# Seven of a layer's sixteen up-projection units computed as seven block products, with the order of the MLP and the home of its side sums changed

## The chip, the cores and the metric

The kernel runs on one core of one Trainium2 chip. The metric is the device time of one execution in microseconds (us). Before the change it is 1293.06 us, the median of three runs from 1291.07 to 1293.43.

## The reference

The reference is a decoder trunk of two layers on 512 tokens of width 1024, in float32. Each layer mixes tokens by attention, then applies a squared-ReLU MLP, then a gated input:

```python
hn = rmsnorm(h, norm_mlp_g[i])
u = jnp.square(jax.nn.relu(hn @ w_mlp_up[i]))      # 1024 -> 4096
h = h + u @ w_mlp_down[i]                          # 4096 -> 1024
gate = jax.nn.sigmoid(rmsnorm(h, norm_ple_g[i]) @ w_ple_gate[i])
h = h + (p[i] @ w_ple_proj[i]) * gate
```

The change lies in the MLP alone, and in a small regrouping of the attention's scratch columns.

## The kernel before, in words

The activations stand transposed: `h[0]` to `h[7]` are eight tiles of 128 features x 512 tokens. Every float32 operand of a matmul is split in two fp32r parts, a high part (ScalarE, a copy) and a low part (VectorE, value minus high part), and each product is three matmuls: high by high, high by low, low by high (`mm3`, L140 to L145). Weights come through `wload` (L112) as 1 MB tiles `raw` (two buffers) and are split into `wh`/`wl` (three buffers each).

The MLP (`mlp`, L734) cuts the 4096 hidden features into four quarters `ch`, and each quarter into four units `c` of 256 features.

`up(ch, c)` (L741) multiplies 256 columns of the up weights with all eight input tiles: 2 x 8 x 3 = 48 matmuls of 512 columns. Then a chain follows in one tile `u` of 7 x 256 columns, of which there is **one buffer** (L747): VectorE applies ReLU and the norm's factor `rstd` (L762), ScalarE squares (L763), VectorE forms four sums and differences (L768, L770, L772), ScalarE takes the high part `uh` of all seven pieces (L774) and VectorE the low part `ul` (L775). The next unit can begin its `u` when `ul` is done.

`down(ch, c)` (L786) multiplies a quarter's hidden features with 256 output columns. It does a 2 x 2 block product with seven block products instead of eight (the Strassen-Winograd scheme): VectorE forms the weights' sums `s13` and `s24` (L799 to L804), they are split (L806), and 7 x 4 x 3 = 84 matmuls of 256 columns run against the seven pieces of `uh`/`ul`. Parts of the result that several outputs share are kept as side sums, eight tiles `sides` in on-chip memory, added up over the quarters by ScalarE and VectorE (`total`, L841) and spread over `h` at the end of the MLP (`side_sums`, L919). VectorE also adds two of the four banks into `h` (L882, L883).

The order of the work is the Tile framework's: it orders each engine's instructions when the kernel is built, in each engine's queue they then run strictly in that order. In the program, quarter `ch + 1` starts with one up unit ahead of quarter `ch`'s four down units, so that the down units never start right behind the last up unit they need (L930 to L937):

```python
for c in range(4):
    up(0, c)
for ch in range(1, NCH):
    up(ch, 0)
    for c in range(4):
        down(ch - 1, c)
    for c in range(1, 4):
        up(ch, c)
```

In the last quarter there is nothing left to put ahead. There `down(3, 0)` multiplies by three of the four hidden units first and by the fourth at the end (`ks`, L863).

Of the kernel before, what the change touches and what calls it, by code (L numbers as in the profile page):

```python
# [35 lines left out]
GROUPS = ((2, 3, 0, 1), (0, 1, 2, 3))  # L36

# [25 lines left out]
def trunk(  # L63
# [29 lines left out]
    def col(name="c"):  # L93
        return spool.tile([P, 1], F32, tag="col", name=nm(name), bufs=24)
# [22 lines left out]
    def wsplit(raw, i, nk, n, pool=None):  # L117
        bufs = 3 if pool is None else 4
# [21 lines left out]
    def mm3(acc, lh, ll, rh, rl, start, stop):  # L140
        mm = nc.tensor.matmul(acc, lh, rh, start=start, stop=False)  # L141
        if warm_end:
            order(mm.ins, warm_end.pop())
        nc.tensor.matmul(acc, lh, rl, start=False, stop=False)  # L144
        return mm.ins, nc.tensor.matmul(acc, ll, rh, start=False, stop=stop).ins  # L145
# [164 lines left out]
    blk0 = [tuple(wpool.tile([P, KT, P], F32R, tag=t, name=nm(t), bufs=3) for t in ("wh", "wl")) for _ in range(2)]  # L310
# [76 lines left out]
    def mixer(layer, norm, nxt):  # L387
# [156 lines left out]
        def soft(hd, bt, i, s):  # L544
# [3 lines left out]
            mn = col("mn")  # L548
# [34 lines left out]
        def attend(g, kind, v, heads):  # L583
# [6 lines left out]
            def weights(x, i, evict):  # L590
                n = P * (i + 1)
                if kind == "diff":
# [3 lines left out]
                    s, r = (spool.tile([P, 2], F32, tag="cols", name=nm("cols"), bufs=12) for _ in range(2))  # L596
                    e0, e1 = (soft(heads[2 * x + m], bias[x][m], i, s[:, m:m + 1]) for m in range(2))
# [7 lines left out]
                if kind == "dil":  # L605
                    if i == 0:
                        bias[x] = load_bias(4 * g + x)
                    s, r = col("s"), col("r")
                    e = soft(heads[x], bias[x], i, s)
# [122 lines left out]
    T1, B11, T3, B21, B22, T2, T4 = range(7)  # L732

    def mlp(layer, fpool, norm, nxt):  # L734
# [3 lines left out]
        sides = [[fpool.tile([P, S], F32, tag=f"side{x}{c}", name=nm("side"), bufs=1) for x in range(2)] for c in range(4)]  # L738
        hidden, spare, stages, b12, low, lows, high = {}, [], [], [], [], [], []

        def up(ch, c):  # L741
            blk = block(w_up[layer, 4 * ch + c], KT, P)
            accs = [ps_wide() for _ in range(2)]
            run(lin_units(accs, blk, ahl, 0, KT, ch == 0 and c == 0))
            if not rstd:
                rstd.append(norm.finish(use_tables(sig_tail) if layer == 0 else None))
            u = fpool.tile([P, 7, HW], F32, tag="u", name=nm("u"), bufs=1)  # L747
            if ch == NCH - 1:
                if c == 0:
# [36 lines left out]
        def down(ch, c):  # L786
# [15 lines left out]
            if last and c:  # L802
                order(sum2, hidden[ch, 3][2] if c == 1 else lows[-1])
# [126 lines left out]
        for c in range(4):  # L930
            up(0, c)
# [236 lines left out]
```

## Time and profile before

| | |
|---|---|
| median of three runs | 1293.06 us |
| the profiled execution | 1293.15 us |
| its span, first to last instruction | 1291.4 us |
| around the span | 1.75 us |
| mean granted TensorE clock | 0.998 |
| layer 0, from the span's start: first up unit's first matmul, first matmul behind the MLP | 270.39 us, 608.25 us |
| layer 1: the same | 895.28 us, 1233.30 us |

A group's row reads: line, engine, operation, result<-operands, then count, busy time, mean of one, and the idle time ahead of it with what ended it. In a row of the timeline the first number is the start, the second the duration (the duration reaches past the next start, since instructions overlap: the pace is read from start to start). TensorE's rows are PE, its weight loads PEld, VectorE DVE, ScalarE ACT, GpSimd POOL, SyncE's DMA queue SPq.

### The profile page before, as it was taken

To read this page: it belongs to the slowest core of one execution; us is meant where nothing else is said; L and a number is where in the kernel's file an instruction comes from. 1 tells how busy PE (TensorE), PEld (TensorE's weight loads), DVE (VectorE), ACT (ScalarE), POOL (GpSimd) and SP (SyncE) were. 2 spreads that over 40 slices of the span, in tenths; PEclk is the share of its full clock that TensorE was granted. 3 is DMA by queue.
4 is the path that set the end of the run, shared out by engine and by line. 5 is a ranking of instruction groups with operands and counts; after the bars stand their busy time and mean duration, and the time that the engine had idled before them with its cause. 6 is when DMAs were issued, how large, how long until landed. Compare 5 with 4: busy or idle time off the path is not lost.

```text
span 1291.4 us, 19228 instructions
## 1 busy us (share of the span) xinstructions
PE 1273.3 (99%) x7488; PEld 1121.0 (87%) x7488; DVE 1003.5 (78%) x1662; ACT 707.8 (55%) x1146; POOL 215.2 (17%) x187
## 2 busy tenths in 40 slices
PE   9999999999999999999999999999999999999997
PEld 7988887888988989989889888788899898898986
DVE  6788898688848869679767777887785885986976
ACT  5667868555535344355556666765553443534644
POOL 2443433500000000001033333222000000000202
PEclk9999999999999999999999999999999999999999
DMA  6421423222232322648332222212223223254751
GB/s 212 144 82 53 161 74 115 90 98 98 98 103 94 119 101 78 194 114 222 130 130 83 82 90 81 67 58 94 102 98 109 87 98 128 69 155 135 173 183 66
DMA packets 33851, 144.25 MB, mean 112 GB/s; under 512 B 3872, under 2 KB 4608, under 8 KB 21088
## 3 DMA queue, kind: packets, MB, share of 16 engines
q1 hardware_dynamic: 29104, 134.37, 30.8%
q0 software_dynamic: 4224, 7.87, 3.6%
q8 instruction: 59, 0.97, 0.3%
q10 hardware_dynamic: 432, 0.79, 0.2%
q14 instruction: 32, 0.26, 0.1%
HBM read 131.92 MB, written 6.37 MB: 107 GB/s over the span
## 4 chain that ended last, share of the span: by engine, by line
PE 84%; DVE 8%; ACT 4%; issue 2%; DMA 1%; SPq 0%; POOL 0%; DVEq 0%; ACTq 0%
PE mm L141 11%; PE mm L144 11%; PE mm L145 11%; PE sc L144 5%; PE sc L145 5%; PE sc L141 5%; PE tp L145 5%; PE pv L145 5%; PE pv L144 5%; PE pv L141 5%; PE tp L144 5%; PE tp L141 5%; PE pv L579 3%; PE tp L558 2%; PE tp L900 2%
## 5 line engine op out<-in xcount | busy, mean ns | idle before, releaser
L122 ACT ACTIVATE wh<-raw 128x1024 fp32r<-128x1024 f32 (+1 forms) x156 | 160.6, 1034 | 140.6 <-PE mm L144 53.1
L126 POOL TENSOR_TENSOR wl<-raw,wh 128x512 fp32r<-128x512 f32 (+1 forms) x132 | 179.8, 1383 | 298.4 <-ACT wh L122 294.6
L141 PE MATMUL mm<-hi,wh 128*128 128x512 f32 x472 | 186.3, 395 | 0.4 <-DVE tmp L495 0.4
L145 PE MATMUL mm<-hi,wl 128*128 128x512 f32 x472 | 184.7, 391 | 0.0
L144 PE MATMUL mm<-lo,wh 128*128 128x512 f32 x472 | 184.5, 391 | 0.0
L128 DVE TENSOR_TENSOR wl<-raw,wh 128x1024 fp32r<-128x1024 f32 x90 | 109.5, 1222 | 38.1 <-ACT wh L122 34.1
L145 PEld LDWEIGHTS mm<-hi,wl 128*128 128x128 f32 x472 | 88.6, 188 | 19.9 <-POOL wl L126 0.4
L141 PEld LDWEIGHTS mm<-hi,wh 128*128 128x128 f32 x472 | 88.7, 188 | 17.2 <-DVE tmp L495 0.8
L144 PEld LDWEIGHTS mm<-lo,wh 128*128 128x128 f32 x472 | 88.7, 188 | 15.7
L784 POOL DMA_DIRECT2D s<-in_w_down_dram x4 | 4.5, 1134 | 581.2 <-DMA s<-in_w_down_dram 290.2
L813 ACT ACTIVATE wh<-s 128x1024 fp32r<-128x1024 f32 x58 | 61.1, 1053 | 54.5 <-DVE s L800 14.9
L552 ACT ACTIVATE e<-e,mn 128x128 f32<-128x128 f32 (+3 forms) x96 | 53.8, 561 | 62.3 <-DVE mn L549 61.9
L775 DVE TENSOR_TENSOR ul<-u,uh 128x1792 fp32r<-128x1792 f32 x32 | 64.8, 2024 | 29.7 <-ACT uh L774 29.6
L814 DVE TENSOR_TENSOR wl<-s,wh 128x1024 fp32r<-128x1024 f32 x58 | 70.8, 1221 | 16.6 <-ACT wh L813 16.2
L774 ACT ACTIVATE uh<-u 128x1792 fp32r<-128x1792 f32 x32 | 54.5, 1702 | 45.5 <-DVE u L772 45.5
L763 ACT ACTIVATE u<-u 128x512 f32<-128x512 f32 x64 | 39.7, 626 | 68.3 <-DVE u L762 68.1
L141 PE MATMUL sc<-hi,wh 128*128 128x512 f32 x184 | 72.2, 392 | 0.5 <-ACT hi L187 0.5
L144 PE MATMUL sc<-lo,wh 128*128 128x512 f32 x184 | 72.0, 391 | 0.4 <-DVE lo L188 0.4
L145 PE MATMUL sc<-hi,wl 128*128 128x512 f32 x184 | 71.7, 390 | 0.0
L141 PE MATMUL mm<-wh,hi 128*128 128x256 f32 (+1 forms) x216 | 63.1, 292 | 0.0
L145 PE MATMUL mm<-wh,lo 128*128 128x256 f32 (+1 forms) x216 | 63.0, 292 | 0.0
L144 PE MATMUL mm<-wl,hi 128*128 128x256 f32 (+1 forms) x216 | 62.9, 291 | 0.0
(306 smaller groups left out, 3873.8 us busy)
## 6 DMA issues: line engine op xcount, KB each, us to landing
raw<-in_w_up_dram SPq DMA_DIRECT2D x32, 1024.0 KB, 4.9
raw<-in_w_down_dram SPq DMA_DIRECT2D x32, 1024.0 KB, 4.9
raw<-in_w_in_dram SPq DMA_DIRECT2D x23, 1024.0 KB, 4.9
raw<-in_w_gate_dram SPq DMA_DIRECT2D x8, 1024.0 KB, 5.4
bias<-urow SPq DMA_DIRECT2D x24, 256.0 KB, 3.9
raw<-in_w_outa_dram SPq DMA_DIRECT2D x8, 768.0 KB, 4.2
pj<-pjd SPq DMA_DIRECT2D x16, 256.0 KB, 4.7
raw<-in_w_proj_dram SPq DMA_DIRECT2D x2, 1024.0 KB, 4.9
```

The costliest lines, as they stand in the source:

```text
L122: act = nc.scalar.activation(hi, src, AF.Copy)
L126: nc.gpsimd.tensor_tensor(lo[:, kx], src[:, kx], hi[:, kx].bitcast(F32), op=ALU.subtract)
L128: last_low[:] = [nc.vector.tensor_tensor(lo, src, hi.bitcast(F32), op=ALU.subtract).ins]
L141: mm = nc.tensor.matmul(acc, lh, rh, start=start, stop=False)
L144: nc.tensor.matmul(acc, lh, rl, start=False, stop=False)
L145: return mm.ins, nc.tensor.matmul(acc, ll, rh, start=False, stop=stop).ins
L552: nc.scalar.activation(e[:, 0:n], e[:, 0:n], AF.Exp, scale=-1.0, bias=mn, accum_out=s)
L763: chain.append(nc.scalar.activation(ui, ui, AF.Square, scale=0.5).ins)
L774: nc.scalar.activation(uh, u, AF.Copy)
L775: part = nc.vector.tensor_tensor(ul, u, uh.bitcast(F32), op=ALU.subtract)
L813: high[:] = [nc.scalar.activation(hi, src, AF.Copy).ins]
L814: low[:] = [nc.vector.tensor_tensor(lo, src, hi.bitcast(F32), op=ALU.subtract).ins]
```

## The change

1. **Seven block products in seven up units.** The units of `SEVEN` (one in quarter 0, three in quarter 1, three in quarter 2) are computed by `up_products` with the scheme that `down` uses: weights' sums, splits of seven weight blocks, 84 matmuls of 256 columns in three accumulators, four copies out of them ("snaps") between the products, and adds on VectorE. Their weights are packed by `_pack4`.
2. **The inputs' combinations.** The scheme needs sums and differences of the input blocks, for each of four pairs of input tiles. `combine_inputs(m)` makes them once a layer, two pairs after `up(0, 0)` and two after `up(0, 1)`, in the tile `u` and its one buffer.
3. **Order.** All four up units of a quarter precede its four down units. The split `ks` of `down`'s first unit now holds in every quarter.
4. **Side sums.** In quarters 0 to 2, `total` copies a bank to a tile `e` (ScalarE) and a DMA from GpSimd's queue writes or adds it to `sides_d` in device memory; the last quarter loads the sums back. The two adds to `h` go the same way, as accumulating DMAs. The tile `e` has five buffers, which the splits of `w11` and the snaps use too.
5. **Buffers.** `wh`/`wl` four instead of three, `uh`/`ul` four instead of five; the attention's columns share tiles; the scratch for GpSimd's DMAs is halved. In the last quarter `down(3, 1)` forms `s13` on VectorE, not by DMA.

The diff, cut to its core:

```diff
+SEVEN = {(0, 2), (1, 0), (1, 1), (1, 2), (2, 0), (2, 1), (2, 2)}
...
+        def differences(u):
+            nc.vector.tensor_tensor(u[:, 0], u[:, 0], u[:, 1], op=ALU.subtract)
+            nc.vector.tensor_tensor(u[:, 1], u[:, 3], u[:, 1], op=ALU.subtract)
+            nc.vector.scalar_tensor_tensor(u[:, 3], u[:, 0], -1.0, u[:, 3], op0=ALU.mult, op1=ALU.subtract)
+            nc.vector.scalar_tensor_tensor(u[:, 2], u[:, 3], -1.0, u[:, 2], op0=ALU.mult, op1=ALU.subtract)
+        def combine_inputs(m):
+            u = fpool.tile([P, 7, HW], F32, tag="u", name=nm("u"), bufs=1)[:, 0:4]
+            for j in range(2):
+                k = 2 * m + j
+                nc.scalar.activation(
+                    u[:, 2 * j:2 * j + 2].rearrange("p a c -> p (a c)"), h[k], AF.Copy, scale=gcol(1, layer, k))
+            differences(u)
+            hi, lo = (fpool.tile([P, 4, HW], F32R, tag=f"{t}{m}", name=nm(t), bufs=1) for t in ("th", "tl"))
+            nc.scalar.activation(hi, u, AF.Copy)
+            nc.vector.tensor_tensor(lo, u, hi.bitcast(F32), op=ALU.subtract)
...
+        def up_products(ch, c, u):
+            rv, s13, s24, _ = quarter_sums(wload(w_up[layer, 4 * ch + c]), None)
+            w11 = split(rv[:, A11:A11 + 1])
+            w12 = split(rv[:, A12:A22 + 1])
+            w24 = split(s24)
+            w13 = split(s13)
...
+            product(run0, w11, 0, B11, True, True)
+            s1 = snap(0, run0)
+            product(first, w12, 0, B21, True, True)
+            product(run0, w24, 0, T2, False, True)
+            s2 = snap(1, run0)
+            nc.vector.tensor_tensor(u[:, B11], first, s1, op=ALU.add)
+            product(second, w13, 0, T1, True, True)
+            r5 = snap(2, second)
+            product(run0, w13, 1, T3, False, True)
+            s3 = snap(3, run0)
+            product(second, w24, 1, B22, False, True)
...
+            product(run0, w12, 1, T4, False, True)
...
+        def collect(dst, src, sign=1.0, add=True):
+            t = t2k("e")[:, 0:src.shape[-1]]
+            nc.scalar.activation(t, src, AF.Copy, scale=sign)
+            nc.gpsimd.dma_start(dst, t, **(dict(accum_op=ALU.add) if add else {}))
...
-            for ks in ((0, 1, 2), (3,)) if last and c == 0 else (range(4),):
+            for ks in ((0, 1, 2), (3,)) if c == 0 else (range(4),):
...
-            nc.vector.tensor_tensor(h[2 * c], h[2 * c], banks[2], op=ALU.add)
+            if last:
+                nc.vector.tensor_tensor(h[2 * c], h[2 * c], banks[2], op=ALU.add)
...
+            else:
+                collect(h[2 * c], banks[2])
+                collect(h[2 * c + 1][:, 0:HW], banks[3][:, 0:HW], -1.0)
...
-        for c in range(4):
-            up(0, c)
-        for ch in range(1, NCH):
-            up(ch, 0)
-            for c in range(4):
-                down(ch - 1, c)
-            for c in range(1, 4):
+        for ch in range(NCH):
+            for c in range(4):
                 up(ch, c)
+                if ch == 0 and c < 2 and SEVEN:
+                    for m in range(2):
+                        combine_inputs(2 * c + m)
...
+            if ch < NCH - 1:
+                for c in range(4):
+                    down(ch, c)
```

What the build makes of it shows in the engines' queues. VectorE, layer 0, from the end of the first up unit's chain on (`ul` with the lowest number) to the second's; `u_...` is always the one buffer, under a new number at each turn. Before:

```order
L775 TENSOR_TENSOR ul_624_3084<-u_622_3082,uh_623_3083 128x1792
L128 TENSOR_TENSOR wl_647_3241<-raw_645_3238,wh_646_3240 128x1024
L762 SCALAR_TENSOR_TENSOR u_632_3154<-sc_630_3104,rstd_574_2889 128x512
L762 SCALAR_TENSOR_TENSOR u_632_3154<-sc_631_3105,rstd_574_2889 128x512
L768 TENSOR_TENSOR u_632_3154<-u_632_3154 128x2x256
L770 SCALAR_TENSOR_TENSOR u_632_3154<-u_632_3154 128x256
```

Now, at the same place, with the chain of the second up unit (L843) behind two turns of the combinations:

```order
L858 TENSOR_TENSOR ul_567_3028<-u_568_3029,uh_566_3027 128x1792
L129 TENSOR_TENSOR wl_612_3291<-raw_610_3288,wh_611_3290 128x1024
L745 TENSOR_TENSOR u_569_3039<-u_569_3039 128x256
L746 TENSOR_TENSOR u_569_3039<-u_569_3039 128x256
L747 SCALAR_TENSOR_TENSOR u_569_3039<-u_569_3039 128x256
L748 SCALAR_TENSOR_TENSOR u_569_3039<-u_569_3039 128x256
L759 TENSOR_TENSOR tl_571_3047<-u_569_3039,th_570_3046 128x1024
L745 TENSOR_TENSOR u_572_3050<-u_572_3050 128x256
L746 TENSOR_TENSOR u_572_3050<-u_572_3050 128x256
L747 SCALAR_TENSOR_TENSOR u_572_3050<-u_572_3050 128x256
L748 SCALAR_TENSOR_TENSOR u_572_3050<-u_572_3050 128x256
L759 TENSOR_TENSOR tl_574_3058<-u_572_3050,th_573_3057 128x1024
```

Two more such turns (`u_585`, `u_588`) stand behind the second unit's chain, then the third up unit's turn, then the fourth's: eight turns of `u` where there were four.

TensorE, layer 0, where the third up unit begins. Before, its matmuls (accumulator `tp_640`) follow the second unit's (`sc_631`) in a row of 48 of 512 columns:

```order
L145 MATMUL sc_631_3105<-hi_600_2989,wl_629_3101 128x512
L141 MATMUL tp_640_3176<-hi_572_2885,wh_636_3168 128x512
L144 MATMUL tp_640_3176<-lo_573_2886,wh_636_3168 128x512
L145 MATMUL tp_640_3176<-hi_572_2885,wl_637_3169 128x512
L141 MATMUL tp_640_3176<-hi_576_2899,wh_636_3168 128x512
```

Now, behind its first two products (24 matmuls that need no combination), the third unit (`tp_605`, `pv_607`) needs the first pair's combination (`th_570`, `tl_571`), and the fourth unit (`pv_615`) is dealt in between:

```order
L146 MATMUL tp_606_3183<-hi_552_2942,wl_600_3171 128x256
L142 MATMUL tp_605_3182<-th_570_3046,wh_601_3174 128x256
L142 MATMUL pv_607_3184<-th_570_3046,wh_603_3178 128x256
L142 MATMUL pv_615_3298<-hi_524_2838,wh_611_3290 128x512
L145 MATMUL pv_615_3298<-lo_525_2839,wh_611_3290 128x512
L145 MATMUL tp_605_3182<-tl_571_3047,wh_601_3174 128x256
L146 MATMUL tp_605_3182<-th_570_3046,wl_602_3175 128x256
L145 MATMUL pv_607_3184<-tl_571_3047,wh_603_3178 128x256
L146 MATMUL pv_607_3184<-th_570_3046,wl_604_3179 128x256
L146 MATMUL pv_615_3298<-hi_524_2838,wl_612_3291 128x512
```

The second, third and fourth pairs' parts (`th_573`, `th_586`, `th_589`) follow in the same manner, each ahead of what is queued behind it; all of the fourth unit and 12 matmuls of the first down unit stand between them. The third unit's last 36 matmuls, and with them its `uh`/`ul`, stand behind the fourth pair.

More of the change, by code (lines that the diff above doesn't have):

```diff
@@ L547, in soft @@
             e = t2k("e")
-            mn = col("mn")
             nc.vector.tensor_tensor_reduce(
@@ L732, in trunk @@
     T1, B11, T3, B21, B22, T2, T4 = range(7)
+    A12, A22, A21, A11 = range(4)
+    sides_d = dpool.tile([DEPTH, 4, 2, P, S], F32, tag="sides", name="sides")
     def mlp(layer, fpool, norm, nxt):
@@ new lines, in mlp @@
+        hidden, sides, b12, low, lows, high, combos = {}, {}, [], [], [], [], []
+        def differences(u):
[13 more added lines that the diff above has]
+            nc.vector.tensor_tensor(lo, u, hi.bitcast(F32), op=ALU.subtract)
+            (h0, l0), (h1, l1) = ahl[2 * m], ahl[2 * m + 1]
+            left, right = slice(0, HW), slice(HW, S)
+            combos.append({T1: (hi[:, 0], lo[:, 0]), T3: (hi[:, 1], lo[:, 1]), T4: (hi[:, 2], lo[:, 2]), T2: (hi[:, 3], lo[:, 3]),
+                           B11: (h0[:, left], l0[:, left]), B21: (h1[:, left], l1[:, left]), B22: (h1[:, right], l1[:, right])})
@@ new lines, in split @@
+        def split(src):
+            n = src.shape[1]
+            if n == 2:
+                hi, lo = (wpool.tile([P, 2, 4, P], F32R, tag=t, name=nm(t), bufs=4) for t in ("wh", "wl"))
+            else:
+                hi, lo = (t2k("e", dtype=F32R).rearrange("p (s k c) -> p s k c", s=1, k=4) for _ in range(2))
+            src = src.rearrange("p s (k c) -> p s k c", k=4)
+            high[:] = [nc.scalar.activation(hi, src, AF.Copy).ins]
+            low[:] = [nc.vector.tensor_tensor(lo, src, hi.bitcast(F32), op=ALU.subtract).ins]
+            return hi, lo
@@ new lines, in up @@
+        def up(ch, c):
+            if (ch, c) not in SEVEN:
+                blk = block(w_up[layer, 4 * ch + c], KT, P)
+                accs = [ps_wide() for _ in range(2)]
+                run(lin_units(accs, blk, ahl, 0, KT, ch == 0 and c == 0))
+                if not rstd:
+                    rstd.append(norm.finish(use_tables(sig_tail) if layer == 0 else None))
+            uh, ul = (fpool.tile([P, 7, HW], F32R, tag=t, name=nm(t), bufs=4) for t in ("uh", "ul"))
+            u = fpool.tile([P, 7, HW], F32, tag="u", name=nm("u"), bufs=1)
+            if (ch, c) in SEVEN:
+                chain = up_products(ch, c, u)
+            else:
+                chain = []
+                for i, acc in enumerate(accs):
+                    ui = u[:, B11 + 2 * i:B11 + 2 * i + 2].rearrange("p a c -> p (a c)")
+                    chain.append(nc.vector.scalar_tensor_tensor(ui, acc, 0.0, rstd[0], op0=ALU.max, op1=ALU.mult).ins)
+                    chain.append(nc.scalar.activation(ui, ui, AF.Square, scale=0.5).ins)
+            if ch == NCH - 1:
+                t = fpool.tile([P, 4, HW], F32R, tag=f"th{c}", name=nm("b12"), bufs=1)
+                hi, lo = t[:, 0], t[:, 1]
+                b12.append((hi, lo))
```

146 lines of the change are left out of this document (65 added, 81 removed).

## The prediction

> **What bounds the kernel now.** First the page: the engines' busy shares, the span in slices, the chain that ended last.
>
> ```profile
> PE 1273.3 (99%) x7488; PEld 1121.0 (87%) x7488; DVE 1003.5 (78%) x1662; ACT 707.8 (55%) x1146; POOL 215.2 (17%) x187
> PE   9999999999999999999999999999999999999997
> DVE  6788898688848869679767777887785885986976
> PEclk9999999999999999999999999999999999999999
> PE 84%; DVE 8%; ACT 4%; issue 2%; DMA 1%; SPq 0%; POOL 0%; DVEq 0%; ACTq 0%
> ```
>
> TensorE is busy in every slice at the full granted clock and holds 84% of the chain. Then the windows of layer 0's MLP, cut where the kind of unit changes (four up units, four down units, again, three down units of the last quarter):
>
> ```profile
> core 0: us, PE busy (x) PEld busy (x) DVE busy (x) ACT busy (x) POOL busy (x), PEclk, DMA share, GB/s
> 365.66:409.22 43.56, 43.56 (x194) 36.04 (x193) 30.62 (x39) 18.32 (x21) 0.00 (x0) 1.00 0.29 97
> 409.22:449.22 40.00, 40.00 (x337) 39.99 (x336) 33.16 (x43) 15.98 (x16) 0.00 (x0) 1.00 0.31 106
> 565.43:596.96 31.53, 30.74 (x254) 30.12 (x253) 28.05 (x45) 19.76 (x26) 6.12 (x7) 1.00 0.64 162
> ```
>
> An up unit takes 43.56 / 4 = 10.89 us (48 matmuls, 0.227 us each from start to start), a down unit 40.00 / 4 = 10.00 us (84 matmuls, 0.119 each). TensorE has no gap but in the last quarter, where three down units should take 30.0 and take 31.5: **1.5 us** lost. So matmuls saved are time saved, as long as VectorE and ScalarE deliver. VectorE is busy 30.62 of 43.56 and 33.16 of 40.00 us: it has slack, no more.
>
> Last the timeline of the first up units, for the anchor points on TensorE (first unit's first matmul, the norm's two matmuls behind it, third unit's first, the first down unit's) and for one turn of the tile `u` on VectorE and ScalarE:
>
> ```profile
> 270.39 0.39 PE L141 MATMUL mm<-hi,wh 128*128 128x512 f32 x1
> 281.52 0.40 PE L262 MATMUL tp<-e,ones_r 128*128 128x512 f32 x1
> 292.70 0.39 PE L141 MATMUL tp<-hi,wh 128*128 128x512 f32 x1
> 325.34 0.28 PE L141 MATMUL sc<-uh,wh 128*128 128x256 f32 x1
> ```
>
> ```profile
> 285.62 0.69 DVE L211 SCALAR_TENSOR_TENSOR rstd<-e,rstd 128x512 f32<-128x512 f32 x1
> 286.35 1.29 DVE L762 SCALAR_TENSOR_TENSOR u<-mm,rstd 128x512 f32<-128x512 f32 x2
> 289.83 0.69 DVE L768 TENSOR_TENSOR u<-u 128x512 f32<-128x512 f32 x1
> 290.55 0.43 DVE L770 SCALAR_TENSOR_TENSOR u<-u 128x256 f32<-128x256 f32 x1
> 291.01 0.42 DVE L772 SCALAR_TENSOR_TENSOR u<-u 128x256 f32<-128x256 f32 x1
> 293.27 2.02 DVE L775 TENSOR_TENSOR ul<-u,uh 128x1792 fp32r<-128x1792 f32 x1 [1.83 <-ACT uh L774]
> 295.21 1.22 DVE L128 TENSOR_TENSOR wl<-raw,wh 128x1024 fp32r<-128x1024 f32 x1
> 296.35 1.28 DVE L762 SCALAR_TENSOR_TENSOR u<-sc,rstd 128x512 f32<-128x512 f32 x2
> 298.32 0.69 DVE L768 TENSOR_TENSOR u<-u 128x512 f32<-128x512 f32 x1 [0.70 <-ACT u L763]
> ```
>
> The first turn of `u` lasts from 286.35 to 295.2, 8.9 us, with a split in between; with nothing in between, by the second turn's rows, it is 1.97 (ReLU, square) + 0.73 + 0.45 + 0.45 + 1.7 (`uh`) + 1.9 (`ul`) = **7.2 us**. `u` has one buffer, so turns follow one another. Four turns of 7 to 9 us fit beside four units of 10.9 us: today they cost nothing, and the extra up unit covers the last one.
>
> **The change, part by part.**
>
> *Matmuls.* A unit with seven products costs 10.00 instead of 10.89 us: 14 x 0.89 = **-12.5 us** for both layers. 84 against 96 half-width matmuls would be an eighth, but the narrow ones cost 0.119, more than half of 0.227.
>
> *The combinations.* This is the term that decides. Each of the four pairs takes `u` for one turn: two copies on ScalarE, four 256-wide operations on VectorE, a 1024-wide high part, a 1024-wide low part. The nearest rows:
>
> ```profile
> 297.12 1.17 ACT L763 ACTIVATE u<-u 128x512 f32<-128x512 f32 x2 [2.94 <-DVE u L762]
> L770 DVE SCALAR_TENSOR_TENSOR u<-u x32: 414/424/427, 290.6 to 1194.5; 128x256 f32<-128x256 f32 x32
> L813 ACT ACTIVATE wh<-s x58: 1041/1060/1067, 314.4 to 1209.3; 128x1024 fp32r<-128x1024 f32 x58
> L814 DVE TENSOR_TENSOR wl<-s,wh x58: 1209/1220/1226, 315.9 to 1210.4; 128x1024 fp32r<-128x1024 f32 x58
> L799 DVE TENSOR_TENSOR s<-raw x24: 678/686/694, 307.9 to 1137.9; 128x512 f32<-128x512 f32 x24
> ```
>
> 1.17 + 1.5 + 1.06 + 1.2 = **4.9 us** a turn. In VectorE's queue two stand behind the first unit's turn and two behind the second's, so on the clock of before, in layer 0:
>
> - `rstd`: VectorE now has four sums (2.5 us) and three splits ahead of it instead of two splits, and one split waits for ScalarE: 2 us later, first turn from 288.3.
> - Turn of unit 0: 8.6, to 296.9. Pair 0 has its high part at 300.6; pairs 0 and 1 are done at 306.7 (2 x 4.9).
> - Turn of unit 1: 7.2, to 313.9. Pairs 2 and 3: 9.8, and 1.0 because ScalarE's next weight split, queued ahead of pair 2's high part, waits for a buffer that the fourth unit's matmuls hold: **324.7**.
>
> TensorE comes to the third unit (seven products) at 292.7, does two products that need no pair, and stands at 295.6 for pair 0: five us. Then it goes in steps, with the fourth unit and 12 matmuls of the first down unit dealt in between. At 324.7 the third unit still has 36 matmuls: 3 x 1.43 us, and two waits for the copies out of its accumulator, to 329.9. Then its own turn of `u`, 8.8 us with two weight splits queued in between, to 338.7, and the fourth unit's, 7.2, to **345.9**. Until then TensorE can do three quarters of the first down unit and parts of the next: 87 of 336 matmuls. The other 249 take 29.6 us, and 2.9 us go at their head (next part): the quarter ends at 378.4. Before it would have ended, without the unit ahead (10.89), at 325.34 - 10.89 + 40.2 = 354.6. **+23.8 us** a layer, its seven-product unit's gain included.
>
> *The order.* With the unit ahead gone, only the split by three and one hidden units covers the last turn: 63 matmuls and 14 of the second unit, 9.2 us, where 10.89 stood before. In quarters 1 and 2 that about suffices. A seven-product unit costs VectorE, by the pace of these rows (0.6 us for 512 columns, 1.14 for 1024), four sums (2.4), splits (4.0), 2.3 of adds and ReLU and 3.2 for the rest, 11.9 us, against 10.0 of TensorE. Three in a row leave it 5.7 behind; the ordinary fourth unit (6.7 against 10.89) and the 9.2 us give that back. Following the queues I find 1.8 us of waits for copies between products and 0.7 at the last turn.
>
> *The side sums by DMA.* TensorE sees none of VectorE's adds that go (33.16 of 40.00 us leaves them hidden), so nothing is gained. The five `e` buffers now carry, for each down unit, the two halves of one split and four tiles that are free when their DMA has landed:
>
> ```profile
> side<-u POOLq DMA_DIRECT2D x8, 256.0 KB, 4.3
> side<-stage POOLq DMA_DIRECT2D x4, 256.0 KB, 5.9
> pjd<-tmp SPq DMA_DIRECT2D x8, 256.0 KB, 3.8
> ```
>
> Within a run of down units the nine products between copy and next use (12.8 us) cover 4.3. Not at the head of a quarter, where the first unit's products all end together: the second unit's split waits 1.7 us for a DMA, and 1.2 for its turn in the queues: 2.4 to 2.9 us a quarter. I take 4.3, an add of the same size from the same queue, though into on-chip memory; 5.9 is the other end. The Trainium skill's page "DMA: Bandwidth & Descriptors", section "Anatomy of one DMA — SWDGE (gpsimd) path", fits 2.0 us + bytes / 436e3, an estimate of 2.6 us here; with it the six waits of 1.7 us would go, and the sum be 10 us lower. The trace has 4.3.
>
> *The last quarter.* Four ordinary units in a row leave VectorE time; I take 1.0 of the 1.5 us as gained. The loads of the sums come 10 us ahead of use.
>
> *The sum*, against the profiled execution's 1293.15 us (0.09 above the median): a layer is +23.8, quarters 1 and 2 each -2.7 + 2.5 + 2.4 = +2.2, quarter 3 -1.0, together +27.2; two layers +54.4. **1347.5 us.**
>
> *Bounds.* With every turn at its least (`rstd` not later, nothing queued in between) the fourth unit's turn ends at 338.9, the quarter at 368.5: +13.9; quarters 1 and 2 at -2.7 each, quarter 3 at -1.5: +7 a layer, 1307. Above: see the third rival.
>
> **The rivals.**
>
> *Hidden after all: 1279.* If `u`'s turns ran beside one another, or TensorE had other work until 324.7, only the matmuls count: -12.5 and -2.0 for the last quarter. For it speaks the page: VectorE has 22% left. Against it, the one buffer and the queues, which are strict. Chance 0.07.
>
> *No change: 1293.* The waits eat just the gain, 6 to 7 us a layer. That is less than even the least chain above. Chance 0.03.
>
> *The chain at its least: 1307 to 1325.* The splits queued between the turns fit into waits for ScalarE. Chance 0.20.
>
> *Heavier: 1357 to 1374.* DMAs land in 5.9 us (+1.6 at six heads, +10), and matmuls are slow when TensorE starts again. The trace shows that once, at the start:
>
> ```profile
> 6.24 0.77 PE L141 MATMUL sc<-hi,wh 128*128 128x512 f32 x1
> 6.86 0.62 PE L144 MATMUL sc<-lo,wh 128*128 128x512 f32 x1
> 7.31 0.40 PE L145 MATMUL sc<-hi,wl 128*128 128x512 f32 x1
> 574.25 0.39 PE L144 MATMUL mm<-ul,wh 128*128 128x256 f32 x1 [0.45 <-DVE ul L775]
> ```
>
> Steps of 0.62 and 0.45 instead of 0.227: 0.6 us a restart; the longest idle within an MLP is 0.45 us (last row), so no row shows what follows 5 us of it. At three long gaps a layer, 5 us of half-speed matmuls, of which half the loss falls on the chain: +5 a layer, +10. One of the two gives 1357, both 1368, and with 0.6 us at some ten shorter stops 1374. Chance 0.25. By the Trainium skill, page "TensorE: Matmul & The Clock Gate", section "What's actually happening", an idle window of about 3.4 us halves the clock until as long a busy one; nothing in this trace shows it, the granted clock is 9 tenths or more in every slice. By that rule this case would be likelier than I make it.
>
> **How the numbers follow.** The forecast's own case has 0.45 and lies at 1335 to 1357. Faster 0.07 and no change 0.03 are left out, and so are the tails of the third and fourth: the range is 1308 to 1374. A measurement of this kernel can tell about 0.2% (2.6 us) from no change; faster 0.07, same 0.03, slower 0.90.
>
> **What would show it.** Right: from the first up unit's first matmul to the last of quarter 0's down units about 108 us in each layer (the same work takes 84 now); in that stretch TensorE's slices fall to 6 or 7 tenths, with waits on ScalarE's `th` and VectorE's `tl`, then on `uh`/`ul`; quarters 1 and 2 stay above 95% busy, seven-product units take 10.0 to 10.7 us. Wrong: TensorE stays at 9 through quarter 0 (first rival), or the loss lies in quarters 1 and 2 with waits on `e` and DMAs (their cost under-rated), or a granted clock under 0.95 there (the fourth rival).

## The result, and the profile after

The changed kernel takes **1411.31 us** (median of four runs, 1404.0 to 1412.03), against 1292.68 in runs of the kernel before on the same chip: a ratio of 1.091 (95% interval 1.087 to 1.094). It is slower, as forecast, but by 118.6 us instead of 54.4, and above the range of 1308 to 1374.

First the page of the changed kernel: engines, the slices of TensorE, VectorE and the granted clock, and the chain that ended last.

```profile
PE 1310.7 (93%) x7992; PEld 1163.4 (83%) x7992; DVE 1058.3 (75%) x1766; ACT 796.4 (56%) x1334; POOL 291.1 (21%) x281
PE   9999999987999998988999999998799989898897
DVE  7788899777696695477867787878677859637766
PEclk9999999998999999999999999999999999999999
PE 37%; issue 24%; DVE 21%; DMA 7%; ACT 6%; POOL 3%; SPq 0%; DVEq 0%; POOLq 0%; ACTq 0%
```

TensorE's share falls from 99 to 93%, several slices show 7 or 8 tenths, and it holds 37% of the chain instead of 84. Then the windows of layer 0's MLP: quarter 0 whole, then up units and down units of quarters 1, 2 and 3 in turn (of quarter 3 the three down units of the prediction's working).

```profile
core 0: us, PE busy (x) PEld busy (x) DVE busy (x) ACT busy (x) POOL busy (x), PEclk, DMA share, GB/s
269.60:379.40 109.80, 93.69 (x567) 83.27 (x566) 83.95 (x113) 58.28 (x78) 10.21 (x15) 0.92 0.31 98
379.40:423.90 44.50, 42.66 (x303) 39.33 (x302) 38.27 (x58) 25.04 (x37) 1.52 (x2) 1.00 0.33 106
423.90:471.30 47.40, 42.61 (x338) 41.52 (x337) 31.55 (x36) 23.99 (x34) 12.31 (x15) 0.96 0.71 157
471.30:515.90 44.60, 43.12 (x302) 39.35 (x301) 38.18 (x58) 25.23 (x37) 1.40 (x2) 1.00 0.34 107
515.90:562.90 47.00, 42.36 (x338) 41.44 (x338) 28.19 (x31) 21.71 (x31) 12.42 (x14) 0.96 0.72 181
562.90:610.30 47.40, 45.35 (x194) 37.07 (x193) 26.00 (x37) 17.89 (x23) 2.56 (x3) 0.96 0.51 140
610.30:655.40 45.10, 36.12 (x253) 35.08 (x252) 32.29 (x50) 22.95 (x31) 7.10 (x8) 0.85 0.51 126
```

Against the 84.2, 83.56, 83.56 and 75.09 us of before (quarter 0 without the unit ahead, as in the prediction's working), this is the loss of one layer by quarter:

| quarter | forecast | measured |
|---|---|---|
| 0 | +23.8 | 109.8 - 84.2 = +25.6 |
| 1 | +2.2 | 44.5 + 47.4 - 83.56 = +8.3 |
| 2 | +2.2 | 44.6 + 47.0 - 83.56 = +8.0 |
| 3 | -1.0 | 47.4 + 45.1 - 75.09 = +17.4 |
| layer | +27.2 | +59.3 |

Quarter 0 came out as forecast. What was missed is 12 us in quarters 1 and 2 together and 18 us in quarter 3. Layer 1, from its first up matmul at 951.86 us to the end of the same stage at 1335.98, takes 384.1 us where it took 326.7 (895.28 to 1222.01): +57.4. The two layers are 117 of the 118.6 us. TensorE's waits in layer 0, the four groups that cost most (us in all, times, longest), show where:

```profile
PE tp L142 <- ACT th L758: 7.8, 3, 4.2
PE mm L146 <- DVE e L784: 6.4, 4, 2.7
PE pv L142 <- ACT wh L783: 3.4, 1, 3.4
PE pv L142 <- ACT uh L857: 2.8, 1, 2.8
```

The first is the forecast wait for the pairs. The second is not: the tiles `e` come late in the down units of quarters 1 and 2. The third lies in quarter 0 too, the fourth at the start of quarter 3's down units. Who waits for the side sums' DMAs, over the whole kernel:

```profile
who waited for it (us, times):
  DVE e L784: 32.1, 12
  DVE h L984: 16.9, 2
  ACT e L871: 13.3, 7
DMA to landing us min/median/max: 2.3/4.7/11.4
```

Of the collecting DMAs alone, from the page's list of DMA issues (KB each, median us to landing):

```profile
sides<-e POOLq DMA_DIRECT2D x48, 256.0 KB, 4.9
```

VectorE stands 32.1 us for tiles `e` that a DMA still holds, and 16.9 us, 8.5 a layer, for a loaded side sum. Two of the former, in quarter 1's down units, from VectorE's timeline:

```profile
440.87 0.69 DVE L784 TENSOR_TENSOR e<-raw,e 128x512 fp32r<-128x512 f32 x1 [1.50 <-DMA sides<-e]
451.29 0.69 DVE L784 TENSOR_TENSOR e<-raw,e 128x512 fp32r<-128x512 f32 x1 [3.93 <-DMA sides<-e]
```

The first, for the second unit's split, is the wait that the prediction put at the head of the quarter (1.7 us there). The second, for the third unit's split, lies inside the run, where the prediction had none, and everything queued behind it on VectorE, the next splits too, stands with it. The DMAs that hold these two tiles, each the first of its row, on GpSimd's queue:

```profile
436.72 0.84 POOL L872 DMA_DIRECT2D sides<-e  x1 [54.20 <-ACT e L871]
443.82 1.73 POOL L872 DMA_DIRECT2D sides<-e  x2 [3.04 <-ACT e L871]
```

VectorE comes to the second tile at 447.36 (451.29 - 3.93), 3.5 us after its DMA was issued, and can write to it 7.5 us after that issue. TensorE's own waits for tiles `e` in quarter 1's down units add up to 3.8 of the 7.4 us that these units lose; the granted clock of 0.96 in their window is, as an estimate, 0.04 x 47.4 = 1.9 more.

Quarter 3, two long waits for a DMA, one of VectorE and one of ScalarE:

```profile
DVE h L984 <- DMA side<-sides: 9.3, 1, 9.3
ACT wh L783 <- DMA s<-in_w_down_dram: 7.3, 1, 7.3
```

The first is the spreading of the sums for outputs 6 and 7 (`side_sums(3)`), which stands in VectorE's queue ahead of the up units' turns of `u`. The second is the DMA that makes `s13` for the third down unit. ScalarE also stands 8.6 us for the weights of an up unit, beside VectorE's wait: SyncE issues these weights behind a load of the sums (more on that queue below).

### The profile page after: what moved, and what is told of

The parts are those of the page before. It is cut to its first block, busy times and chain, and to the rows that moved or that the text cites. A ratio compares the mean times of both kernels' runs of the same rounds, so it can differ in the third digit from the quotient of the medians.

```text
span 1409.7 us, 20936 instructions
## 1 busy us (share of the span) xinstructions
PE 1310.7 (93%) x7992; PEld 1163.4 (83%) x7992; DVE 1058.3 (75%) x1766; ACT 796.4 (56%) x1334; POOL 291.1 (21%) x281
## 4 chain that ended last, share of the span: by engine, by line
PE 37%; issue 24%; DVE 21%; DMA 7%; ACT 6%; POOL 3%; SPq 0%; DVEq 0%; POOLq 0%; ACTq 0%
PE mm L142 7%; PE mm L146 7%; PE mm L145 7%; DVE wl L784 3%; DMA sides<-e 2%; PE pv L579 2%; DVE ul L858 2%; POOL h L872 2%; PE tp L558 2%; POOL sides L872 2%; DVE wl L129 1%; ACT uh L857 1%; PE pv L145 1%; PE pv L142 1%; PE pv L146 1%
## 5 line engine op out<-in xcount | busy, mean ns | idle before, releaser
L142 PE MATMUL mm<-hi,wh 128*128 128x512 f32 (+1 forms) x456 | 177.6, 390 | 4.8 <-ACT wh L783 2.0
L146 PE MATMUL mm<-hi,wl 128*128 128x512 f32 (+1 forms) x456 | 175.3, 384 | 1.1 <-DVE wl L129 1.1
L145 PE MATMUL mm<-lo,wh 128*128 128x512 f32 (+1 forms) x456 | 174.7, 383 | 0.0
L872 POOL DMA_DIRECT2D sides<-e x48 | 38.9, 836 | 506.8 <-ACT e L871 504.3
L784 DVE TENSOR_TENSOR wl<-s,wh 128x1024 fp32r<-128x1024 f32 x88 | 107.3, 1220 | 41.7 <-ACT wh L783 41.6
L783 ACT ACTIVATE wh<-s 128x1024 fp32r<-128x1024 f32 x88 | 92.5, 1056 | 80.9 <-DVE s L771 33.7
L129 DVE TENSOR_TENSOR wl<-raw,wh 128x1024 fp32r<-128x1024 f32 x62 | 75.0, 1218 | 31.7 <-ACT wh L123 31.1
L552 ACT ACTIVATE e<-e,cols 128x128 f32<-128x128 f32 (+3 forms) x96 | 53.8, 561 | 59.5 <-DVE cols L549 59.1
L857 ACT ACTIVATE uh<-u 128x1792 fp32r<-128x1792 f32 x32 | 54.4, 1699 | 45.2 <-DVE u L855 45.2
L146 PE MATMUL sc<-hi,wl 128*128 128x512 f32 (+1 forms) x176 | 66.9, 380 | 2.4 <-DVE wl L129 2.4
L142 PE MATMUL sc<-hi,wh 128*128 128x512 f32 (+1 forms) x176 | 67.1, 381 | 0.0
L145 PE MATMUL sc<-lo,wh 128*128 128x512 f32 (+1 forms) x176 | 66.9, 380 | 0.2 <-DVE lo L189 0.2
L142 PE MATMUL pv<-uh,wh 128*128 128x256 f32 x184 | 53.4, 294 | 14.0 <-ACT uh L857 7.2
```

Of the source, the lines that this page charges most:

```text
L129: last_low[:] = [nc.vector.tensor_tensor(lo, src, hi.bitcast(F32), op=ALU.subtract).ins]
L142: mm = nc.tensor.matmul(acc, lh, rh, start=start, stop=False, skip_group_check=again)
L145: nc.tensor.matmul(acc, lh, rl, start=False, stop=False, skip_group_check=again)
L552: nc.scalar.activation(e[:, 0:n], e[:, 0:n], AF.Exp, scale=-1.0, bias=mn, accum_out=s)
L783: high[:] = [nc.scalar.activation(hi, src, AF.Copy).ins]
L784: low[:] = [nc.vector.tensor_tensor(lo, src, hi.bitcast(F32), op=ALU.subtract).ins]
```

## The experiments

The theory after the trace: separate causes add up, the turns of `u` in quarter 0, tiles `e` held by DMAs in quarters 1 and 2, two waits for DMAs in quarter 3. The first rival: TensorE cools down at one gap and the rest follows. The second: VectorE, ScalarE or the DMAs' traffic are the limit, not buffers and places in queues. All runs in one table; the quarters are layer 0's, in the profiled execution, with quarter 0 counted from 270.4 us on in every row (for the changed kernel that is 109.0 us, where its window above, from 269.6, has 109.8). The profiled execution is not always a typical one: for "one each" it took 1303.65 us and for "two, loads last" 1302.45, in both cases the slowest of all; for "one, loads last" 1289.13, among the fastest.

| kernel | us | ratio to before (95%) | quarters 0, 1, 2, 3 (us) |
|---|---|---|---|
| changed | 1411.31 | 1.087 to 1.094 | 109.0, 91.9, 91.6, 92.5 |
| no seven products | 1338.07 | 1.032 to 1.037 | 82.9, 84.6, 84.8, 92.1 |
| pairs apart | 1385.56 | 1.070 to 1.077 | 101.7, 88.7, 94.9, 87.6 |
| h by VectorE | 1367.93 | 1.057 to 1.061 | 108.1, 83.1, 83.1, 86.1 |
| e relieved | 1385.14 | 1.071 to 1.075 | 108.5, 83.1, 85.4, 90.0 |
| last quarter | 1395.39 | 1.077 to 1.083 | 110.1, 90.0, 92.3, 84.4 |
| sums behind | 1386.57 | 1.071 to 1.077 | 109.3, 91.8, 89.3, 79.3 |
| three mended | 1323.41 | 1.024 to 1.027 | 98.7, 83.1, 82.7, 76.6 |
| six units | 1307.43 | 1.011 to 1.014 | 90.2, 82.1, 83.1, 77.4 |
| pairs late | 1302.36 | 1.007 to 1.009 | 86.7, 83.1, 83.1, 77.3 |
| none mended | 1295.43 | 1.001 to 1.004 | 83.3, 83.7, 83.7, 74.4 |
| one each | 1297.20 | 1.003 to 1.007 | 87.0, 82.8, 82.9, 77.4 |
| one, loads last | 1292.27 | 0.999 to 1.001 | 87.2, 82.9, 81.8, 73.5 |
| two, loads last | 1297.83 | 1.003 to 1.006 | 88.8, 82.2, 82.1, 73.5 |
| kept warm 1 | 1339.73 | 1.036 to 1.040 | 82.2, 85.6, 85.0, 91.1 |
| kept warm 2 | 1345.34 | 1.041 to 1.043 | 82.9, 84.6, 87.1, 87.9 |

**One part undone at a time.** First, all seven products undone:

```diff
-SEVEN = {(0, 2), (1, 0), (1, 1), (1, 2), (2, 0), (2, 1), (2, 2)}
+SEVEN = set()
```

> No up unit uses seven products, so no pair is combined and no snaps are taken; the new order, the side sums in device memory and the last quarter stay as in the changed kernel. Theory 1 (four separate causes: turns of the tile u in series in quarter 0, tiles e held by DMAs in quarters 1 and 2, two waits for DMAs in quarter 3): quarter 0 loses nearly all of its 25.6 us a layer (to about +3), quarters 1 and 2 lose the matmul gain but keep their slow down units (+7 each, 47 instead of 40 us), quarter 3 keeps +17: 34 us a layer, 1361 us. Theory 2 (the pairs' gap starts everything: TensorE cools down there and the rest follows): all quarters go back, 1295 to 1310 us.

1338.07 us, between the two. Quarter 0 gets all of its loss back and quarter 3 keeps its own, as theory 1 says. But quarters 1 and 2 recover too, where I had expected their down units to stay at 47 us: they take 41.1 with the very DMAs of the changed kernel, which are no faster here (6.4 us in the median to landing, 4.9 there); VectorE stands 5.0 us for tiles `e` in the whole kernel instead of 32.1. So the short supply of tiles `e` hurts much only together with the seven-product units. These use the tiles too, and they give VectorE more to do; which of the two matters was not tried apart.

Then the pairs, in tiles of their own:

```diff
-            u = fpool.tile([P, 7, HW], F32, tag="u", name=nm("u"), bufs=1)[:, 0:4]
+            u = temps[m % 2][:, 0:4]
...
+        temps = [fpool.tile([P, 7, HW], F32, tag=t, name=nm("temp"), bufs=4) for t in ("uh", "ul")]
```

> The pairs of inputs are combined in two tiles of their own (two buffers of uh and ul that quarter 0 does not need yet) instead of the tile u; all the work is the same, u has four turns in quarter 0 instead of eight. Theory 1 (the turns of the one buffer set quarter 0): the pairs are done near 311 instead of 324.7 us, the quarter ends some 12 us earlier, and the kernel takes 1387 us; the other quarters stay. Theory 2 (VectorE and ScalarE are too busy there, the buffer does not matter): less than 4 us a layer, 1403 to 1411 us.

1385.56, theory 1's 1387, but in part by luck: of the 12.1 us that layer 0 gains by the table, quarter 0 has 7.3 and quarter 3, which the edit does not touch, 4.9. The one buffer is a part of quarter 0's loss of 25.6 us, not all of it.

Then the adds to `h`, by VectorE straight from the banks as before the change:

```diff
-            if last:
-                nc.vector.tensor_tensor(h[2 * c], h[2 * c], banks[2], op=ALU.add)
...
-            else:
-                collect(h[2 * c], banks[2])
-                collect(h[2 * c + 1][:, 0:HW], banks[3][:, 0:HW], -1.0)
+            nc.vector.tensor_tensor(h[2 * c], h[2 * c], banks[2], op=ALU.add)
...
```

> In quarters 0 to 2 the two banks that belong to h are added by VectorE as before the change, not by a copy to e and an accumulating DMA; the side sums still go by DMA. Theory 1 (tiles e wait for their DMAs, and the VectorE queue stands behind them): the down units of quarters 1 and 2 fall from 47 to about 43 us, and the loads of the sums in quarter 3 start earlier (about 5 us): 13 us a layer, 1385 us. Theory 2 (VectorE is the short one in the down units and the granted clock does the rest): two more adds of 0.7 and 0.4 us a unit, 1411 to 1425 us.

1367.93: 43 us back, more than theory 1 said. The down units of quarters 1 and 2 in its windows, VectorE now with more work (35.27 us instead of 31.55 in the first) and TensorE at full clock:

```profile
419.98:461.52 41.54, 40.49 (x337) 39.80 (x336) 35.27 (x44) 21.70 (x28) 6.82 (x8) 1.00 0.64 147
503.04:544.58 41.54, 40.52 (x337) 39.75 (x336) 30.70 (x37) 19.90 (x26) 7.04 (x9) 1.00 0.66 165
```

That takes copies, DMAs and bytes away at once. The next kernel takes away only demands on `e`: one of a down unit's four copies gets small tiles of its own.

```diff
-            t = t2k("e")[:, 0:src.shape[-1]]
+            n = src.shape[-1]
+            t = fpool.tile([P, HW], F32, tag="half", name=nm("half"), bufs=3) if n == HW else t2k("e")
```

> The changed kernel, in which the half-width adds to h (one of four collecting copies of a down unit) take three small tiles of their own instead of a tile e; all copies, DMAs and bytes stay. Theory 1 (the number of tiles e limits the down units): their e is asked for five times a unit instead of six; quarters 1 and 2's down units fall from 47 to 43 to 45 us and the kernel to 1390 to 1403 us. Theory 2 (the DMAs' traffic or ScalarE's and VectorE's work is what slows them): 1408 to 1414 us.

1385.14, 26 us back, below theory 1's range. The same windows:

```profile
420.69:462.01 41.32, 40.44 (x337) 39.77 (x335) 31.54 (x36) 24.36 (x35) 12.29 (x15) 1.00 0.73 168
504.78:547.43 42.65, 40.15 (x338) 39.27 (x336) 28.09 (x31) 21.93 (x32) 11.30 (x15) 1.00 0.72 172
```

VectorE's work (31.54 and 31.55 us), ScalarE's and the DMAs' share (0.73 and 0.71) are those of the changed kernel, and still the down units take 41.3 instead of 47.4 us. In the down units of quarters 1 and 2 the number of tiles was the limit, not the traffic.

**The last quarter.** The edit was to remove both waits; it removed only that for `s13`:

```diff
-            rv, s13, s24, sum2 = quarter_sums(raw, add_up(src) if last and c != 1 else None)
+            rv, s13, s24, sum2 = quarter_sums(raw, add_up(src) if last and c not in (1, 2) else None)
...
-        side_sums(3)
         for c in range(3):
             down(NCH - 1, c)
+            if c == 1:
+                side_sums(3)
```

> Only the last quarter is changed: the sums for the outputs 6 and 7 are spread behind the second down unit instead of ahead of the first, and the third down unit forms s13 on VectorE instead of by DMA. Theory 1 (VectorE stands 9.3 us behind the load of a side sum, and ScalarE 7.3 us behind the DMA that makes s13): quarter 3 gets back 6 to 13 of its 17 us, the kernel takes 1385 to 1399 us. Theory 2 (these waits lie beside others; a granted clock of 0.85 to 0.96 and slow transfers set the quarter): under 4 us a layer, 1403 to 1411 us.

1395.39, at theory 1's upper edge. VectorE's timeline says why no more: the sums stand where they stood, since a later place in the program does not bind the order of the queue.

```profile
581.72 0.42 DVE L984 TENSOR_TENSOR h<-h,side 128x256 f32<-128x256 f32 x1 [9.49 <-DMA side<-sides]
```

So they were tied to the last up unit's low part:

```diff
-        side_sums(3)
         for c in range(3):
             down(NCH - 1, c)
+            if c == 0:
+                side_sums(3, [hidden[NCH - 1, 3][2], *low])
```

> As the kernel with the changed last quarter, which took 1395.4 us, but the sums for outputs 6 and 7 are tied behind the low part of the last up unit (there they had still come early in VectorE's queue and had waited 9.5 us). Theory 1 (that wait holds up every turn of u in quarter 3): quarter 3's up units take 43.6 to 44.5 us instead of 45.2, its down units 34 to 36 instead of 39.1, 1381 to 1388 us. Theory 2 (the weights, queued behind the loads of the sums on SyncE, are late whatever VectorE does): 1392 to 1397 us.

1386.57, theory 1. The up units and then the down units of quarter 3:

```profile
560.84:604.38 43.54, 43.54 (x194) 36.03 (x193) 24.02 (x31) 18.04 (x23) 2.84 (x4) 1.00 0.59 160
604.38:640.16 35.78, 31.82 (x254) 30.90 (x252) 32.59 (x53) 21.58 (x27) 6.05 (x7) 0.95 0.50 126
```

43.5 and 35.8 where the changed kernel has 47.4 and 45.1.

**Together.** The three repairs in one kernel (pairs apart, `h` by VectorE, sums behind):

> All three repairs together: the pairs in two tiles of their own, the adds to h by VectorE, the last quarter with s13 on VectorE and the sums behind the last up unit. Theory 1 (separate causes that add up): 1411.3 - 25.7 - 43.4 - 16 to 25, that is 1317 to 1326 us. Theory 2 (the repairs meet the same waits): 1335 to 1350 us. What is left above the time before then lies in quarter 0, whose third unit still waits for the pairs (some 17 us a layer).

1323.41. The single gains are 25.7 + 43.4 + 24.7 = 93.8 us; together they are 87.9. The causes are separate, nearly.

**What is left of the products.** From here each kernel holds the repairs of `h` and of the last quarter. First, quarter 0's third unit an ordinary one, so that no pair is needed before quarter 1:

> As the kernel with all three repairs, but the third unit of quarter 0 is an ordinary one again (six seven-product units a layer), so the pairs are not needed before quarter 1. Theory 1 (TensorE waits in quarter 0 because the third unit needs the pairs at once): quarter 0 ends some 17 us earlier, 34 us below the kernel with the three repairs: 1283 to 1293 us. Theory 2 (the pairs' work on VectorE and ScalarE makes the up units' own turns late all the same): only 5 to 10 us a layer, 1300 to 1315 us.

1307.43: theory 2. Quarter 0 falls to 90.2, not to 82. So the pairs were moved behind quarter 0's last up unit, into `u` again, beside the down units:

```diff
-                if ch == 0 and c < 2 and SEVEN:
-                    for m in range(2):
-                        combine_inputs(2 * c + m)
+                if ch == 0 and c == 3 and SEVEN:
+                    for m in range(4):
+                        combine_inputs(m)
```

> Six units with seven products and the three repairs, but the pairs are combined behind quarter 0's last up unit, in the tile u again, beside the down units, where VectorE has room. Theory 1 (in the kernel with six units, 1307.4 us, the pairs delay the up units' own turns by some 7 us a layer): quarter 0 takes 83 to 84 instead of 90 us, 1292 to 1296 us. Theory 2 (the pairs cost as much beside the down units, whose splits they delay): 1300 to 1308 us.

1302.36, theory 2 again. The window of quarter 0's down units, with the pairs beside them:

```profile
314.03:357.12 43.09, 40.74 (x338) 39.89 (x337) 41.12 (x63) 29.98 (x39) 4.55 (x8) 1.00 0.40 139
```

VectorE is busy 41.12 of 43.09 us: here too the pairs are work for an engine that has almost no time to spare. And the same with no seven products:

> No seven products in up units, the adds to h by VectorE, the last quarter with s13 on VectorE and its sums behind the last up unit: what the new order and the side sums in device memory cost by themselves once their waits are mended. Theory 1 (the lost up unit ahead still leaves a gap at the head of each quarter's down units, 1 to 2 us): 1303 to 1308 us. Theory 2 (order and side sums are free then): 1290 to 1296 us.

1295.43, theory 2: order and side sums cost 0.2% once their waits are mended. My theory of a gap at every head fell: quarters 1 and 2 take 83.7 us as before (83.56). It also says that six units with seven products are a loss of 7 us, where 6 x 2 x 0.89 = 10.7 had to be gained. With one such unit in quarters 1 and 2 each:

> As the kernel with six seven-product units and late pairs (1302.4 us), but only the first up unit of quarters 1 and 2 has seven products. Theory 1 (three in a row leave VectorE behind, so the down units start late, 41.5 us instead of 40.1, and give back what the up units gain): the down units of quarters 1 and 2 fall to 40.1 to 40.4 us and the up units take 42.8 to 43.0; the pairs' 3 us in quarter 0 stay: 1297 to 1301 us. Theory 2 (a seven-product unit's gain holds, the loss lies elsewhere): slower than with six, 1306 to 1310 us.

1297.20, theory 1: the down units take 40.1 and 40.2 us, so a single unit keeps its gain. But quarter 3's down units still take 33.84 us (in an execution 6 us above the median), and with no such unit 30.86. SyncE's queue in this kernel shows a candidate; the rows are a load of sums, weights, a load, weights:

```profile
518.23 2.50 SPq L994 DMA_DIRECT2D side<-sides  x2
520.83 0.38 SPq L115 DMA_DIRECT2D raw<-in_w_up_dram  x1
532.10 0.32 SPq L994 DMA_DIRECT2D side<-sides  x1
532.52 0.37 SPq L115 DMA_DIRECT2D raw<-in_w_up_dram  x1
```

From 520.83 to 532.10 SyncE issues nothing: a load of the sums waits for the DMA that still adds to them, and weights stand behind it. The loads were tied behind the last quarter's weights:

```diff
-                        nc.sync.dma_start(sides[c, x], sides_d[layer, c, x])
+                            d = nc.sync.dma_start(sides[k, x], sides_d[layer, k, x])
+                            order(d.ins, up_loads[-1])
```

> As the kernel with one seven-product unit in each of quarters 1 and 2 (1297.2 us), but SyncE issues the eight loads of the side sums behind all weights of the last quarter's up units, not between them. Theory 1 (a load that waits for a collecting DMA holds up the weights queued behind it, VectorE's first turn of u in quarter 3 then starts 3 us late and the down units take 33.8 instead of 30.9 us): 2.5 to 3 us a layer, 1291 to 1293 us. Theory 2 (VectorE's lag there has another cause): 1296 to 1299 us.

1292.27, theory 1; the down units of quarter 3:

```profile
565.85:595.75 29.90, 29.90 (x253) 29.77 (x252) 28.90 (x49) 18.82 (x24) 6.08 (x7) 1.00 0.61 154
```

TensorE has no gap there, and the kernel stands level with the one before (0.999 to 1.001). With two units a quarter:

> The same with two seven-product units in each of quarters 1 and 2. Theory 1 (two in a row leave VectorE little behind, each is worth its 0.7 to 0.9 us as long as the head of the down units stays covered): 1288 to 1292 us, the first kernel to beat the one before. Theory 2 (the second one is given back at the head of the down units): 1291 to 1295 us, no gain on one unit.

1297.83, neither. The down units keep their pace (40.1 in both quarters), but behind the MLP a new wait stands, here in layer 0, and the same in layer 1:

```profile
613.56 0.77 PE L144 MATMUL mm<-hi,wh 128*128 128x512 f32 x1 [4.37 <-DVE h L966]
```

Over both layers it is 8.4 us, in an execution of 1302.45 us. Whether the kernel would lie below the one before without it is not shown: 1302.45 - 8.4 = 1294.05 is still above 1292.08, and what the slow clock behind the wait adds was not measured. Why the gate's input comes late here and not with one unit was not tried. No kernel here beats the one before.

**The clock.** Behind a gap TensorE runs slowly, and its windows show 0.85 to 0.96 for whole stages. What that costs by itself was tried on the kernel without seven products, where only quarter 3 is slow: idle matmuls in the gaps, so that the clock stays up while no wait becomes shorter.

```diff
+            def spin(n, behind):
+                for i in range(n):
+                    d = nc.tensor.matmul(banks[3][:, HW:S], us[0][0][:, B11, 0:P], us[0][0][:, T1], start=True, stop=True).ins
...
```

> The kernel without seven products in up units (1338.1 us), in whose last quarter TensorE waits twice a layer for some 4 us and then runs at a granted clock of 0.5; here idle matmuls of 256 columns fill these two waits (38 behind the first pass of the first down unit, 28 behind the second down unit; they write a half bank that nothing reads). Nothing else is changed, no wait is shorter. Theory 1 (the slow clock behind a gap is a cost of its own, about 2.6 us a gap): the three down units of quarter 3 take 41 to 43 instead of 46.7 us and the kernel 1327 to 1331 us. Theory 2 (VectorE and ScalarE set the pace behind the gap as before it, so TensorE's clock does not matter): 1336 to 1340 us.

1339.73, no change. But 38 of a layer's 66 idle matmuls stood in the wrong place: the gap lies ahead of the third hidden unit's matmuls, not of the fourth's, so one gap stayed. Again, with these in the gap (the diff above is this second form):

> As the first attempt on the kernel without seven products (1338.1 us), but the 38 idle matmuls now stand where the gap is: in the first down unit of the last quarter, ahead of its first matmul on the third hidden unit, which waits 4.39 us; the 28 others stay ahead of the third down unit, where they had filled the gap of 3.94 us (behind it the clock stayed at 1.00 and the unit took 9.5 us). Theory 1 (a slow clock behind a gap is a cost of its own, some 2.6 us each): no granted clock of 0.50 is left in that quarter, its three down units take 41 to 42.5 instead of 46.7 us, the kernel 1326 to 1331 us. Theory 2 (the engines that feed TensorE set the pace there): at least 45.5 us, 1335 to 1340 us.

1345.34 us, and 44.4 for the stage: neither. Theory 1 had 41 to 42.5 us for the stage and at most 1331 for the kernel, theory 2 at least 45.5 and at most 1340. Quarter 3's down units, first without, then with the idle matmuls:

```profile
568.12:614.84 46.72, 35.70 (x253) 34.56 (x252) 32.93 (x52) 24.16 (x32) 7.11 (x8) 0.85 0.48 120
```

```profile
568.54:612.90 44.36, 39.65 (x320) 38.09 (x319) 29.57 (x44) 20.52 (x26) 5.39 (x6) 1.00 0.44 107
```

The clock is at 1.00, the matmuls proper take 39.65 - 66 x 0.12 = 31.7 us instead of 35.7, but the stage is only 2.4 us shorter: 1.6 of the 4.0 come back as waits. So the slow clock has a price of its own in this stage, 2.4 of the 4.0 us that the matmuls lose by it. The whole kernel gains nothing; its ratio to before is 1.042, and 1.035 without the idle matmuls. Other places of this profile are longer (quarter 2's down units by 2.3, the first unit behind the MLP by 5.0); what moved those is open.

## Why the prediction was wrong, step by step

*What bounds the kernel* and *the matmuls*: right. With `h` added by VectorE, the up units of quarter 1 take 83.1 - 41.54 = 41.5 instead of 43.56 us, 2.0 of the 2.7 counted (in the changed kernel itself they take 44.5).

*The combinations*: right in place and size. TensorE stood at 294.6 (forecast 295.6), the third and fourth units' turns of `u` ended at 340.3 and 347.8 (338.7 and 345.9), the quarter at 379.4 (378.4). The reason was too narrow. I put it down to the eight turns of one buffer; with the pairs in tiles of their own about a third of the loss goes, without a unit that needs them at once another third, and of the rest a good part is VectorE's plain work for the pairs: 3.4 us even beside the down units (86.7 against 83.3).

*The order*: about right. With `h` added by VectorE, which leaves the seven-product units as they are, quarters 1 and 2 take 83.1 us, 0.5 less than before; the terms without the DMAs, -2.7 + 2.5, had 0.2 less. The order by itself costs next to nothing: with no products at all these quarters take 83.7.

*The side sums by DMA*: the step that failed. I wrote that within a run of down units "the nine products between copy and next use (12.8 us) cover 4.3" and put a wait at the head alone. The head's wait was right (1.50 us in quarter 1 for 1.7). But 12.8 us is a distance in TensorE's products, and the next to use the tile is VectorE, which splits weights ahead of their product: it came 3.5 us after the DMA's issue and had to wait until 7.5. Six demands a unit on five tiles turn the ring (the tiles handed out one after the other) in 5/6 of 10 us, 8.3 on average, and the collecting DMAs took 4.9 us in the median and up to 11.4, not 4.3 always. So waits came inside the run, and the queue behind the waiting VectorE made them longer. For quarters 1 and 2 of a layer the term was 2 x 2.4 = 4.8 us; relieving `e` of one demand in six returned 15.0 in layer 0 (91.9 + 91.6 - 83.1 - 85.4), of two, with their DMAs, 17.3. The short ring is not the whole of it: without seven-product units the same six demands cost these down units 1.1 us (41.1 against 40.0), and what in those units makes it dear stays open. The Trainium skill's page "DMA: Bandwidth & Descriptors", section "Anatomy of one DMA — SWDGE (gpsimd) path", would have made the term smaller still, by its fit an estimate of 2.6 us; the trace has 4.9.

*The last quarter*: failed too. "The loads of the sums come 10 us ahead of use" held for the issue that I saw in the program, not for the queue: the last load waits for a DMA whose copy waited for a tile `e` (ScalarE stood 9.7 us for it), and VectorE, with the spreading of the sums early in its queue, stood 9.3 us. That `s13`, with one buffer, would be late, I had not priced. These waits' removal returned 24.7 us, against a forecast gain of 2.

*The rivals*: "heavier" was right that DMAs and the clock would cost more, but not where or how much. Its DMAs were to cost 10 us at the six heads; they cost more, and inside the runs. It had the slow clock at +5 a layer; by the granted clock of the windows it is at most 0.08 x 109.8 + 0.04 x (47.4 + 47.0 + 47.4) + 0.15 x 45.1 = 21 us a layer, an estimate. How much of that lengthens the kernel was tested in one stage of another kernel, which gave 2.4 of 7.0, and is open for the others. The slow clock follows from the gaps: in the kernel with the three repairs, none of which touches it, the mean granted clock is 0.987 instead of 0.970. Of the signs I gave for being wrong, waits on `e` and DMAs in quarters 1 and 2 appeared; a granted clock under 0.95 did not there (0.96), but it did in quarters 0 and 3.

## What to carry to other kernels

For a ring of buffers that a DMA empties, compare the time in which the demands turn it round with the slowest landing, and measure the distance to the next use in the queue of the engine that uses the buffer next, not in that of the engine that ends up with the result. If the ring is short, one demand fewer can be worth more than faster work; here it was, beside the seven-product units, and cost little without them. An instruction that waits for a DMA early in an engine's strict queue costs what stands behind it, on the compute engines and on the queue that issues weights alike, and to name a later place in the program does not move it unless the order is tied. Work saved on the busiest engine is paid for on the next: here 0.89 us of matmuls a unit against pairs, sums and splits on a VectorE that had a fifth to spare on average, and in quarter 0 got 84 us of work where the whole quarter had taken 84.

## What was not expected of the hardware

The clock falls after shorter gaps than thought. In quarter 0, TensorE's rows around the first wait, and the granted clock by stretches of 2 us:

```profile
294.56 0.28 PE L146 MATMUL tp<-hi,wl 128*128 128x256 f32 x1
299.01 0.58 PE L142 MATMUL tp<-th,wh 128*128 128x256 f32 x1 [4.17 <-ACT th L758]
299.61 0.63 PE L142 MATMUL pv<-hi,wh 128*128 128x512 f32 x1
300.03 0.63 PE L145 MATMUL pv<-lo,wh 128*128 128x512 f32 x1
300.46 0.41 PE L145 MATMUL tp<-tl,wh 128*128 128x256 f32 x1
```

```profile
296.00:298.00 2.00, 0.00 (x0) 0.00 (x0) 1.64 (x5) 0.36 (x2) 0.00 (x0) 0.83 0.00 0
300.00:302.00 2.00, 2.00 (x8) 1.63 (x7) 1.02 (x3) 1.33 (x2) 0.00 (x0) 0.50 0.00 0
304.00:306.00 2.00, 2.00 (x11) 1.70 (x10) 1.82 (x2) 0.11 (x1) 0.00 (x0) 0.96 0.00 0
```

The wide matmuls step by 0.42 us (299.61 to 300.03) instead of 0.227, at a granted clock of 0.50, until 304. By the Trainium skill, page "TensorE: Matmul & The Clock Gate", section "What's actually happening", an idle window of about 3.4 us brings this half clock; here it does. But a gap of 2.03 us in quarter 1 did the same:

```profile
464.22 0.39 PE L146 MATMUL mm<-uh,e 128*128 128x256 f32 x1 [2.03 <-DVE e L784]
464.95 0.41 PE L142 MATMUL mm<-uh,e 128*128 128x256 f32 x1
465.17 0.41 PE L145 MATMUL mm<-ul,e 128*128 128x256 f32 x1
```

0.22 us a step instead of 0.119. On this point the page and the trace differ, and the trace decides: two microseconds can be enough. They need not be: behind a gap of 2.48 us in layer 1 (restart at 1230.38) the matmuls step by 0.12 from the second on.
